# Softmax of the attention stage: a chained scaled minimum as bias, and the row sum's reciprocal as a power on GpSimd

## Chip, cores, metric

The kernel runs on one core of a Trainium2 chip, as one launch. The metric is device microseconds of one execution, the median of several runs. Five engines work side by side, each through its own instruction queue in order, and wait for one another by semaphores: TensorE (PE; its weight loads are PEld), VectorE (DVE), ScalarE (ACT), GpSimd (POOL), SyncE (SP, which here only issues DMAs).

## The reference

One layer of a hybrid block: 16 meta tokens and 1024 tokens (1040 rows, width 1024) go through a norm, then a "forgetting attention" and a diagonal state-space model side by side, then a gated merge, an output projection and a gated convolutional feed-forward. What the change touches is the attention, 8 heads of 64:

```
log_f = log_sigmoid(f_logit + b_forget);  cum_f = cumsum(log_f)
s = (q . k) / sqrt(64) + cum_f[t] - cum_f[s]        # s <= t, else -1e30
p = softmax(s, axis=-1)
out = p @ v
```

`cum_f[t]` is the same along a row, so it falls out of the softmax, and the kernel adds only the term of the key.

## The kernel before

All products are float32 made of two parts: a value is split into a high half (`hi`, rounded to the matmul type) and a low half (`lo`, what is left), and three matmuls make one product. The split is the pair that stands all over the trace: a copy on ScalarE to the high half and a subtraction on VectorE for the low half (`split_lo`, L125).

The program goes through its stages one after the other: norm, state-space model, gates, the gated linear unit, values, **attention** (about 378 to 645 us of the span), merge, output projection, norm, feed-forward. In attention the outer loop runs over four pairs of heads, the inner one over ten units of a pair: one unit for the 16 meta tokens of each head, then four units per head of two chunks of 128 queries each. A pair has 18 chunks, the stage 72. `scores(...)` of a unit is called before `second(...)` (which calls `pv`) of the unit before it, so that a unit's softmax runs while PE works at something else.

`scores` does this for a chunk of 128 queries and `kc` keys (16, 144, 272, ... 1040):

- GpSimd copies the queries to `qz` (L620) and cuts the mask into the diagonal block of the forget row: `fm` (L622, affine select).
- PE makes the scores into a PSUM tile `sp` (two buffers), in one to three blocks of at most 512 keys (L632, L633).
- VectorE goes over each block in one or two pieces (the part left of the diagonal with `fb`, the diagonal with `fm`): L638 adds the forget term, writes the sum to `pt` and the piece's largest value to a column of `mx`. In the trace that is a CUSTOM_DVE and a DVE_READ_ACCUMULATOR2 for each piece. A chunk has one to four pieces, all chunks together 184.
- VectorE takes the largest of the columns (L643, where there is more than one: 64 chunks) and multiplies it by -0.125 (L644): `nm[:, 1]`.
- ScalarE computes exp(0.125 * pt + nm) with the row sum (L645, an ACTIVATE and an ACTIVATION_READ_ACCUMULATOR).
- VectorE takes the reciprocal of the sum (L646), GpSimd multiplies the row by it (L647).

`pv` then takes the groups of one or two key blocks: PE transposes them to `tp` (L675), ScalarE casts `tp` to `th` (L682), VectorE subtracts to `tl` (L125), PE multiplies with the values: the high half (L696, reads `th`) and the low half (L697, reads `tl`), both into `po`. Between groups `fill` hands PE projection matmuls (L145 to L147, tile `mm`) of the next pair's queries and keys and of the merge gates; their weights are split by GpSimd (L135 `whi`, L125 `wlo`), and GpSimd also finishes the gates (L365 `gs`).

The order of instructions on each engine is not the order of the code: the framework's scheduler lists them by its own simulated timeline, under the data dependencies and a few manual ones ("spread", which ties the fill matmuls to marks a few groups back).

Of the kernel before, what the change touches and what calls it, by code (L numbers as in the profile page):

```python
# [9 lines left out]
F = mybir.dt.float32  # L10
# [3 lines left out]
AF = mybir.ActivationFunctionType  # L14
ALU = mybir.AluOpType
AX = mybir.AxisListType
# [3 lines left out]
P = 128  # L20
# [27 lines left out]
def block_kernel(ctx, tc, x, meta, g1, w_q, w_k, w_v, w_f, w_u, w_g, b_f, w_ao, lam_d, bw_d, cw_d,  # L48
                 d_sk, l_dt, w_glu, w_o, g2, w_up, cwt_d, w_dn, gf, out, dbg=None, upto=99):
    nc = tc.nc  # L50
    dbg = dbg or {}
    out = out[0]

    V, S, GP, PE, SY = nc.vector, nc.scalar, nc.gpsimd, nc.tensor, nc.sync

    def pool(stack, name, bufs=1, side=None, **k):
        return stack.enter_context(
            tc.tile_pool(name=name, bufs=bufs, side=side, reuse_waits="tile", **k))

    cp = pool(ctx, "const", side="left")  # L60
# [7 lines left out]
    def mm_ps():  # L68
        mm_n[0] += 1
        if mm_n[1] and mm_n[0] % 4 == 0:  # L70
            return po_ps()
        return pp.tile([P, 512], F, tag="mm", name="mm", bufs=3)
# [4 lines left out]
    def s_ps(name="sp"):  # L77
        return pp.tile([P, 512], F, tag="sp", name=name, bufs=2)
# [9 lines left out]

    ident = cp.tile([P, P], F, name="ident")
    make_identity(nc, ident)  # L90
    nhalf = cp.tile([P, 1], F, name="nhalf")
    V.memset(nhalf, -0.5)
    one = cp.tile([P, 1], F, name="one")
    V.memset(one, 1.0)


    u_d = dp.tile([SW // P, P, P // GC, NCH], F, name="u_d")
# [506 lines left out]
    ap = pool(st_a, "attn", side="left")  # L604
# [6 lines left out]
    def scores(t_, e, c, fb):  # L611
        t, n = TILES[c]
        kc = KS[c]
        Qs, Ks = t_[f"q{e}"], t_[f"k{e}"]
        hr = slice(64 * e, 64 * e + 64)
        m_ = max(n, 32)
        dg = kc - n

        qz = qzero[e][c % 2]
        GP.tensor_copy(qz[hr, :m_], Qs[hr, t:t + m_].bitcast(F))  # L620
        fm = ap.tile([P, P], F, tag="fm", name="fm", bufs=2)
        GP.affine_select(out=fm[:n, :n], in_=fb[:n, dg:kc], pattern=[[-1, n]],  # L622
                         compare_op=ALU.is_ge, fill=-1e30, base=0, channel_multiplier=1)
        pt = ap.tile([P, L], F, tag="pt", name="pt", bufs=4)
        mx = ap.tile([P, 4], F, tag="mx", name="mx", bufs=4)
        nb = -(-kc // 512)
        w = -(-kc // nb // 8) * 8
        ns = 0
        for b in range(nb):
            a0, a1 = b * w, min(kc, b * w + w)  # L630
            ps = s_ps()
            PE.matmul(ps[:m_, :a1 - a0], Qs[:, t:t + m_], Ks[:, a0:a1], start=True, stop=False)  # L632
            PE.matmul(ps[:m_, :a1 - a0], qz[:, :m_], t_["kl"][:, a0:a1], start=False, stop=True)  # L633
            for lo, hi, src in ((a0, min(a1, dg), fb), (max(a0, dg), a1, None)):
                if hi <= lo:
                    continue
                s_ = fb[:n, lo:hi] if src is not None else fm[:n, lo - dg:hi - dg]
                V.tensor_tensor_reduce(out=pt[:n, lo:hi], in0=ps[:n, lo - a0:hi - a0], in1=s_, scale=1.0,  # L638
                                       scalar=-3e38, op0=ALU.add, op1=ALU.max, accum_out=mx[:n, ns:ns + 1])
                ns += 1  # L640
        nm = ap.tile([P, 4], F, tag="nm", name="nm", bufs=4)
        if ns > 1:
            V.reduce_max(nm[:n, 0:1], mx[:n, :ns], axis=AX.X)  # L643
        V.tensor_scalar(nm[:n, 1:2], nm[:n, 0:1] if ns > 1 else mx[:n, :1], -0.125, None, ALU.mult)  # L644
        S.activation(pt[:n, :kc], pt[:n, :kc], AF.Exp, bias=nm[:n, 1:2], scale=0.125, accum_out=nm[:n, 2:3])  # L645
        V.reciprocal(nm[:n, 3:4], nm[:n, 2:3])  # L646
        GP.tensor_scalar(pt[:n, :kc], pt[:n, :kc], nm[:n, 3:4], 1.0, ALU.mult, ALU.mult)  # L647
        return pt

    def pv(h, cs, pts, ob):  # L650
# [81 lines left out]
    for pr in range(H // 2):  # L732
# [46 lines left out]
        for cs, e in units:  # L779
            pts = [scores(qk, e, c, fbs[e]) for c in cs]  # L780
            if prev:
                second(*prev)
            prev = (cs, e, pts)
# [47 lines left out]
    for i in range(KD):  # L831
# [3 lines left out]
        for t, n in QBLK:  # L835
            ps = mm_ps()
# [27 lines left out]
    for hf in range(2):  # L864
        woh, wol = wo[hf]
        sl = slice(512 * hf, 512 * hf + 512)
        for c, (t, n) in enumerate([(T0, 2)] + TILES[1:]):
            dst = hm if c == 0 else h2[:, c - 1]
            ps = mm_ps()
# [747 lines left out]
```

## Time and profile before

| | |
|---|---|
| median of 3 runs | 1508.43 us (1506.48 to 1508.51) |
| the profiled execution | 1508.38 us, of which the span of its instructions is 1506.6 us |
| PE busy | 1453.2 us, 96% of the span (weight loads 1366.2, 91%) |
| DVE busy | 1063.1 us, 71%, 2243 instructions |
| ACT busy | 677.9 us, 45% |
| POOL busy | 681.9 us, 45%, 759 instructions |
| chain that ended last, by engine | PE 80%, DVE 8%, DMA 3%, issue 3%, POOL 2%, ACT 2% |

How to read it: a share of busy time is a mean over stages. An engine that is busy for less than the whole of a stage costs time only where something waits for it, and what waits is read from the chain of work that ended last (which goes back from the last instruction, at each step to what released it) and from the idle times with what ended them. Matmuls are pipelined, so a row of PE overlaps the next, and a small gap can hide behind the end of the one before. The time of an execution is about 1.8 us more than its span.

### The profile page before, as it was taken

To read this page: it belongs to the slowest core of one execution; us is meant where nothing else is said; L and a number is where in the kernel's file an instruction comes from. 1 tells how busy PE (TensorE), PEld (TensorE's weight loads), DVE (VectorE), ACT (ScalarE), POOL (GpSimd) and SP (SyncE) were. 2 spreads that over 40 slices of the span, in tenths; PEclk is the share of its full clock that TensorE was granted. 3 is DMA by queue.
4 is the path that set the end of the run, shared out by engine and by line. 5 is a ranking of instruction groups with operands and counts; after the bars stand their busy time and mean duration, and the time that the engine had idled before them with its cause. 6 is when DMAs were issued, how large, how long until landed. Compare 5 with 4: busy or idle time off the path is not lost.

```text
span 1506.6 us, 26221 instructions
## 1 busy us (share of the span) xinstructions
PE 1453.2 (96%) x9637; PEld 1366.2 (91%) x9637; DVE 1063.1 (71%) x2243; ACT 677.9 (45%) x1322; POOL 681.9 (45%) x759
## 2 busy tenths in 40 slices
PE   5999998999999999999999899999999999989997
PEld 4999997998999999999778899999999999778885
DVE  7989567861657676656255988888777775788785
ACT  6256555531646565532033444444444444444333
POOL 2010004760645555525011644555543326599766
PEclk9999999999999999999999999999999999999998
DMA  5365642551021202157241146776642214873413
GB/s 213 86 152 154 140 123 87 165 159 41 28 74 49 78 24 91 43 190 256 88 163 61 51 111 161 196 190 185 162 124 84 79 63 162 302 228 126 139 44 112
DMA packets 82805, 187.74 MB, mean 125 GB/s; under 512 B 13594, under 2 KB 26538, under 8 KB 82324
## 3 DMA queue, kind: packets, MB, share of 16 engines
q1 hardware_dynamic: 68180, 155.49, 31.5%
q0 software_dynamic: 8704, 19.98, 7.5%
q10 hardware_dynamic: 5792, 10.60, 1.9%
q8 instruction: 76, 1.25, 0.3%
q14 instruction: 53, 0.43, 0.1%
HBM read 146.95 MB, written 60.96 MB: 138 GB/s over the span
## 4 chain that ended last, share of the span: by engine, by line
PE 80%; DVE 8%; DMA 3%; issue 3%; POOL 2%; ACT 2%; SPq 0%; POOLq 0%; ACTq 0%; DVEq 0%
PE mm L147 5%; PE mm L145 5%; PE mm L146 5%; PE sp L202 4%; PE sp L201 4%; PE sp L203 4%; PE tp L201 3%; PE tp L202 3%; PE tp L203 3%; PE mm L203 3%; PE mm L201 3%; PE mm L202 3%; PE tp L675 2%; PE po L697 2%; PE po L696 2%
## 5 line engine op out<-in xcount | busy, mean ns | idle before, releaser
L145 PE MATMUL mm<-xhi,whi 128*128 128x342 f32 (+2 forms) x584 | 191.6, 329 | 1.0 <-DVE q L125 1.0
L146 PE MATMUL mm<-xlo,whi 128*128 128x342 f32 (+2 forms) x584 | 190.1, 326 | 1.4 <-DVE xlo L125 1.4
L147 PE MATMUL mm<-xhi,wlo 128*128 128x342 f32 (+2 forms) x584 | 190.6, 327 | 0.4 <-DMA wlo<-in_w_g_dram 0.4
L146 PEld LDWEIGHTS mm<-xlo,whi 128*128 128x128 f32 x584 | 111.2, 190 | 2.1 <-DVE xlo L125 1.7
L145 PEld LDWEIGHTS mm<-xhi,whi 128*128 128x128 f32 x584 | 111.2, 191 | 1.9 <-PE sp L633 0.8
L147 PEld LDWEIGHTS mm<-xhi,wlo 128*128 128x128 f32 x584 | 111.0, 190 | 1.3 <-DMA wlo<-in_w_g_dram 0.6
L958 POOL TENSOR_TENSOR ov<-ov,og 128x1024 f32<-128x1024 f32 x21 | 51.3, 2442 | 130.7 <-ACT og L957 127.9
L125 DVE TENSOR_TENSOR sw<-sf,sw 128x512 fp32r<-128x512 f32 x76 | 70.7, 930 | 53.3 <-ACT sw L927 53.1
L927 ACT CAST sw<-sf 128x512 fp32r<-128x512 f32 x76 | 47.4, 624 | 113.1 <-POOL sf L935 82.1
L201 PE MATMUL mm<-xhi,sw 128*128 128x256 f32 (+1 forms) x304 | 85.4, 281 | 0.8 <-DVE ov L982 0.8
L203 PE MATMUL mm<-xhi,sw 128*128 128x256 f32 (+1 forms) x304 | 85.5, 281 | 0.0
L202 PE MATMUL mm<-xlo,sw 128*128 128x256 f32 (+1 forms) x304 | 85.2, 280 | 0.0
L682 ACT CAST th<-tp 128x256 fp32r<-128x256 f32 (+3 forms) x120 | 56.1, 472 | 62.1 <-PE tp L675 29.1
L125 DVE TENSOR_TENSOR tl<-tp,th 128x256 fp32r<-128x256 f32 (+3 forms) x120 | 65.2, 547 | 25.9 <-ACT th L682 24.5
L927 ACT CAST sw<-raw 128x512 fp32r<-128x512 f32 x69 | 42.3, 620 | 87.1 <-DMA raw<-in_w_up_dram 36.5
L1018 DVE SCALAR_TENSOR_TENSOR ov<-hv,cwt,ov 128x1024 f32<-128x1024 f32 x38 | 76.8, 2021 | 0.4 <-ACT ov L1016 0.4
L647 POOL TENSOR_SCALAR pt<-pt,nm 128x144 f32<-128x144 f32 (+4 forms) x72 | 51.0, 710 | 52.9 <-DVE nm L646 51.7
L935 POOL TENSOR_TENSOR sf<-raw,sf 128x512 f32<-128x512 f32 x38 | 62.7, 1649 | 23.0 <-DVE sw L125 23.0
L935 POOL TENSOR_TENSOR sf<-raw 128x512 f32<-128x512 f32 x38 | 50.6, 1332 | 48.2 <-DMA raw<-in_w_up_dram 20.4
L645 ACT ACTIVATE pt<-pt,nm 128x144 f32<-128x144 f32 (+4 forms) x72 | 52.9, 736 | 26.0 <-DVE nm L644 25.6
L638 DVE CUSTOM_DVE_ANT_0 pt<-sp,fb 128x328 f32<-128x328 f32 (+8 forms) x112 | 46.4, 430 | 20.6 <-PE sp L633 12.2
L163 POOL TENSOR_TENSOR rs<-vr,nhalf 128x1 f32<-128x1 f32 (+2 forms) x18 | 10.5, 594 | 110.1 <-PE mm L879 52.4
(589 smaller groups left out, 5444.2 us busy)
## 6 DMA issues: line engine op xcount, KB each, us to landing
raw<-in_w_up_dram SPq DMA_DIRECT2D x44, 512.0 KB, 3.8
t_d<-in_w_dn_dram POOLq DMA_DIRECT2D x44, 256.0 KB, 6.9
ar<-a_d SPq DMA_DIRECT2D x44, 256.0 KB, 4.6
wr<-t_d SPq DMA_DIRECT2D x44, 256.0 KB, 2.9
a_d<-ov SPq DMA_DIRECT2D x21, 512.0 KB, 2.6
wr<-in_w_dn_dram SPq DMA_DIRECT2D x33, 256.0 KB, 3.6
t_d<-in_w_dn_dram SPq DMA_DIRECT2D x22, 256.0 KB, 4.6
t_d<-t_d SPq DMA_DIRECT2D x22, 256.0 KB, 4.9
```

The source lines that it names most:

```text
L125: return eng.tensor_tensor(out_, src, hi.bitcast(F), ALU.subtract)
L145: yield PE.matmul(ps, whi[:, i, :], ahi[:, i], start=(i == 0), stop=False)
L146: yield PE.matmul(ps, whi[:, i, :], alo[:, i], start=False, stop=False)
L147: yield PE.matmul(ps, wlo[:, i, :], ahi[:, i], start=False, stop=(i == k - 1))
L201: PE.matmul(ps, a[0][:, i], bh, start=(i == 0 and not joins), stop=False, skip_group_check=True)
L202: PE.matmul(ps, a[0][:, i], bl, start=False, stop=False, skip_group_check=True)
L203: PE.matmul(ps, a[1][:, i], bh, start=False, stop=(i == kh - 1), skip_group_check=True)
L645: S.activation(pt[:n, :kc], pt[:n, :kc], AF.Exp, bias=nm[:n, 1:2], scale=0.125, accum_out=nm[:n, 2:3])
L682: S.copy(th[:kn, z:tw], tp[:kn, z:tw])
L927: S.copy(hi, src)
L935: sums.append(GP.tensor_tensor(f_, a, b, op))
L1018: V.scalar_tensor_tensor(out=o, in0=h_[:, j:SEQ + j], scalar=cwc(j, m), in1=o, op0=ALU.mult, op1=ALU.add)
```

## The change

The scores' pieces are now scaled by -0.125 as they leave PSUM, and each takes a running minimum: a piece starts from the column that the piece before it wrote (the first from 3e38) and writes its own. The last column is the minimum of the whole row, which is the negated scaled maximum, and goes into the exponential as its bias directly; the scale there is -1. The reduction over the columns and the multiplication by -0.125 are gone. The reciprocal of the row sum is now a power with exponent -1 on GpSimd, ahead of the multiplication that uses it. The constants are one tile of three columns.

```diff
-    nhalf = cp.tile([P, 1], F, name="nhalf")
-    V.memset(nhalf, -0.5)
-    one = cp.tile([P, 1], F, name="one")
-    V.memset(one, 1.0)
+    consts = cp.tile([P, 3], F, name="consts")
+    nhalf, one, minus = (consts[:, i:i + 1] for i in range(3))
+    for c_, v_ in ((nhalf, -0.5), (one, 1.0), (minus, -1.0)):
+        V.memset(c_, v_)
...
-                V.tensor_tensor_reduce(out=pt[:n, lo:hi], in0=ps[:n, lo - a0:hi - a0], in1=s_, scale=1.0,
-                                       scalar=-3e38, op0=ALU.add, op1=ALU.max, accum_out=mx[:n, ns:ns + 1])
+                V.tensor_tensor_reduce(out=pt[:n, lo:hi], in0=ps[:n, lo - a0:hi - a0], in1=s_, scale=-0.125,
+                                       scalar=mx[:n, ns - 1:ns] if ns else 3e38, op0=ALU.add, op1=ALU.min,
+                                       accum_out=mx[:n, ns:ns + 1])
                 ns += 1
-        nm = ap.tile([P, 4], F, tag="nm", name="nm", bufs=4)
-        if ns > 1:
-            V.reduce_max(nm[:n, 0:1], mx[:n, :ns], axis=AX.X)
-        V.tensor_scalar(nm[:n, 1:2], nm[:n, 0:1] if ns > 1 else mx[:n, :1], -0.125, None, ALU.mult)
-        S.activation(pt[:n, :kc], pt[:n, :kc], AF.Exp, bias=nm[:n, 1:2], scale=0.125, accum_out=nm[:n, 2:3])
-        V.reciprocal(nm[:n, 3:4], nm[:n, 2:3])
-        GP.tensor_scalar(pt[:n, :kc], pt[:n, :kc], nm[:n, 3:4], 1.0, ALU.mult, ALU.mult)
+        nm = ap.tile([P, 2], F, tag="nm", name="nm", bufs=4)
+        S.activation(pt[:n, :kc], pt[:n, :kc], AF.Exp, bias=mx[:n, ns - 1:ns], scale=-1.0, accum_out=nm[:n, :1])
+        GP.tensor_tensor(nm[:n, 1:2], nm[:n, :1], minus[:n], ALU.pow)
+        GP.tensor_scalar(pt[:n, :kc], pt[:n, :kc], nm[:n, 1:2], 1.0, ALU.mult, ALU.mult)
```

The changed file is two lines shorter: the exponential is L643 there, the power L644, the row's multiplication L645, the transposes L673, the products L694 and L695. Outside the attention stage the order on every engine is the same but for the constants' writes at the start; in it the scheduler lists much anew. Two engines, three places:

GpSimd, near the end of the first pair of heads, around the row of 1040 keys of the first head (`pt_4895` before, `pt_4867` now; `whi` and `wlo` are a projection's weights, `gs` a gate). Before:

```order
L680 MEMSET th_4972 128x128
L681 MEMSET tl_4973 128x128
L647 TENSOR_SCALAR pt_4895<-pt_4895,nm_4910 128x1040
L365 TENSOR_SCALAR gs_4837<-gs_4837 128x1026
L125 TENSOR_TENSOR wlo_5461<-raw_5458,whi_5460 128x1024
L620 CAST qz11_4146<-q1_4156 64x128
```

Now:

```order
L679 MEMSET tl_4943 128x128
L644 TENSOR_TENSOR nm_4882<-nm_4882,consts_71 128x1
L365 TENSOR_SCALAR gs_4811<-gs_4811 128x1026
L125 TENSOR_TENSOR wlo_5417<-raw_5414,whi_5416 128x1024
L645 TENSOR_SCALAR pt_4867<-pt_4867,nm_4882 128x1040
L620 CAST qz11_4146<-q1_4156 64x128
```

The power has the place of the multiplication, and the gate and the weights' low half now go between the two.

PE, in the first pair, where the rows of 400 and 528 keys of the first head are transposed (`tp_4509` and `tp_4516` before, `tp_4491` and `tp_4498` now; the products read the casts, `th_4418` of the unit before, `th_4494` of `tp_4491`). Before:

```order
L675 MATMUL tp_4516<-ident_66,pt_4379 128x128
L675 MATMUL tp_4509<-ident_66,pt_4397 128x128
L675 MATMUL tp_4516<-ident_66,pt_4397 128x128
L675 MATMUL tp_4516<-ident_66,pt_4379 128x128
L675 MATMUL tp_4516<-ident_66,pt_4397 128x128
L696 MATMUL po_4414<-th_4418,vt_3860 128x256
L697 MATMUL po_4414<-tl_4419,vt_3860 128x256
L696 MATMUL po_4414<-th_4426,vt_3860 128x256
```

Now:

```order
L673 MATMUL tp_4491<-ident_66,pt_4369 128x128
L673 MATMUL tp_4498<-ident_66,pt_4369 128x128
L673 MATMUL tp_4491<-ident_66,pt_4385 128x128
L673 MATMUL tp_4498<-ident_66,pt_4385 128x128
L673 MATMUL tp_4498<-ident_66,pt_4369 128x128
L673 MATMUL tp_4498<-ident_66,pt_4385 128x128
L694 MATMUL po_4490<-th_4494,vt_3860 128x256
L695 MATMUL po_4490<-tl_4495,vt_3860 128x256
```

Before, the products of the unit ahead stood behind the transposes; now the products of the same tile do, both halves within four instructions of its last transpose.

PE, at the start of the last unit's products, at the end of the stage (`tp_8376` before and `tp_8240` now are the second group, whose casts are `th_8381` and `th_8245`). Before, from the last three of the seven projection matmuls that follow `tp_8376`:

```order
L145 MATMUL mm_8408<-xhi_90,whi_8274 128x342
L146 MATMUL mm_8408<-xlo_91,whi_8274 128x342
L147 MATMUL mm_8408<-xhi_90,wlo_8275 128x342
L675 MATMUL tp_8394<-ident_66,pt_8208 128x128
L675 MATMUL tp_8394<-ident_66,pt_8230 128x128
L675 MATMUL tp_8394<-ident_66,pt_8208 128x128
L675 MATMUL tp_8394<-ident_66,pt_8230 128x128
L696 MATMUL po_8368<-th_8372,vt_3860 128x256
L697 MATMUL po_8368<-tl_8373,vt_3860 128x256
L696 MATMUL po_8368<-th_8381,vt_3860 128x256
L697 MATMUL po_8368<-tl_8382,vt_3860 128x256
```

Now, from the last transpose of `tp_8240`:

```order
L673 MATMUL tp_8240<-ident_66,pt_8096 128x128
L146 MATMUL mm_8272<-xlo_91,whi_8138 128x342
L147 MATMUL mm_8272<-xhi_90,wlo_8139 128x342
L694 MATMUL po_8232<-th_8236,vt_3860 128x256
L695 MATMUL po_8232<-tl_8237,vt_3860 128x256
L673 MATMUL tp_8258<-ident_66,pt_8076 128x128
L673 MATMUL tp_8258<-ident_66,pt_8096 128x128
L673 MATMUL tp_8258<-ident_66,pt_8076 128x128
L673 MATMUL tp_8258<-ident_66,pt_8096 128x128
L694 MATMUL po_8232<-th_8245,vt_3860 128x256
L695 MATMUL po_8232<-tl_8246,vt_3860 128x256
```

Two projection matmuls are left between the group's transposes and what follows, where there were seven.

## Rows read from the trace of the kernel before

**Rows 1.** Engines' busy time in stretches (from:to us, busy us and instructions), attention stage.

```profile
core 0: us, PE busy (x) PEld busy (x) DVE busy (x) ACT busy (x) POOL busy (x), PEclk, DMA share, GB/s
378.00:645.00 267.00, 264.16 (x1840) 257.33 (x1839) 175.06 (x767) 154.66 (x375) 147.43 (x304) 1.00 0.17 55
```

**Rows 2.** Chain of work that ended last, 378 to 645 us, shares by line.

```profile
by line: PE mm L147 17.6%; PE mm L145 17.3%; PE mm L146 17.1%; PE tp L675 13.5%; PE po L696 8.4%; PE po L697 8.4%; PE sp L632 6.3%; PE sp L633 6.2%; DVE tl L125 1.3%; DVE q L125 1.1%; ACT th L682 1.0%; issue 0.8%; DVE pt L638 0.4%; ACT q L4
```

**Rows 3.** Instructions on tile `nm` (count: duration ns least/median/most).

```profile
L646 DVE RECIPROCAL nm<-nm x72: 141/164/168, 380.7 to 641.1; 128x1 f32<-128x1 f32 x64, 16x1 f32<-16x1 f32 x8
L643 DVE TENSOR_REDUCE nm<-mx x64: 131/152/158, 381.3 to 639.5; 128x1 f32<-128x3 f32 x32, 128x1 f32<-128x2 f32 x24, 128x1 f32<-128x4 f32 x8
L644 DVE TENSOR_SCALAR nm<-nm x64: 130/153/155, 381.5 to 639.6; 128x1 f32<-128x1 f32 x64
```

**Rows 4.** Instructions of L638, its accumulator reads: one for each piece.

```profile
L638 DVE DVE_READ_ACCUMULATOR2_ANT mx<- x184: 71/83/86, 378.4 to 639.3; 128x1 f32 x176, 16x1 f32 x8
```

**Rows 5.** Who waited for whom, 378 to 645 us (us in total, times, longest).

```profile
POOL pt L647 <- DVE nm L646: 51.7, 40, 5.3
...
DVE nm L646 <- ACT pt L645: 24.4, 42, 1.3
```

**Rows 6.** Instructions of L163, the norms' power on GpSimd.

```profile
L163 POOL TENSOR_TENSOR rs<-vr,nhalf x18: 549/554/1109, 10.7 to 816.6; 128x1 f32<-128x1 f32 x16, 16x1 f32<-16x1 f32 x1, 2x1 f32<-2x1 f32 x1
```

**Rows 7.** VectorE in order of time (start us, us), one chunk's last pieces.

```profile
467.86 0.08 DVE L638 DVE_READ_ACCUMULATOR2_ANT mx<- 128x1 f32 x1
467.86 0.28 DVE L638 CUSTOM_DVE_ANT_0 pt<-sp,fm 128x128 f32<-128x128 f32 x1
468.07 0.08 DVE L638 DVE_READ_ACCUMULATOR2_ANT mx<- 128x1 f32 x1
468.19 0.16 DVE L643 TENSOR_REDUCE nm<-mx 128x1 f32<-128x3 f32 x1
```

**Rows 8.** All engines in order of time, one row of 272 keys from exponential to transpose.

```profile
453.96 0.18 ACT L645 ACTIVATION_READ_ACCUMULATOR pt<-pt,nm 128x1 f32 x1
...
454.17 0.16 DVE L646 RECIPROCAL nm<-nm 128x1 f32<-128x1 f32 x1 [0.34 <-ACT pt L645]
...
454.94 0.49 POOL L647 TENSOR_SCALAR pt<-pt,nm 128x272 f32<-128x272 f32 x1
...
457.05 0.38 PE L675 MATMUL tp<-ident,pt 128*128 128x128 f32 x2
```

**Rows 9.** Chain in order of time, 415.5 to 418 us: a group of 256 columns.

```profile
415.47 0.16 PE mm L147
...
416.04 0.12 PE tp L675
...
416.24 0.38 ACT th L682
...
416.65 0.44 DVE tl L125
...
417.13 0.39 PE po L697
```

**Rows 10.** The same, 448.8 to 451 us: a group of 512 columns.

```profile
449.13 0.59 ACT th L682
...
449.74 0.70 DVE tl L125
...
450.87 0.12 PE po L696
```

**Rows 11.** GpSimd at the end of the first pair, and PE's first transpose of its row.

```profile
429.88 1.16 POOL L647 TENSOR_SCALAR pt<-pt,nm 128x1040 f32<-128x1040 f32 x1
430.99 1.09 POOL L365 TENSOR_SCALAR gs<-gs 128x1026 f32<-128x1026 f32 x1
432.01 2.43 POOL L125 TENSOR_TENSOR wlo<-raw,whi 128x1024 fp32r<-128x1024 f32 x1
...
434.05 0.38 PE L675 MATMUL tp<-ident,pt 128*128 128x128 f32 x2
```

## The prediction

> **What bounds the kernel now.** I read the page first: TensorE is busy for 96% of the span and holds 80% of the chain that ended last. So a saving on another engine is worth something only where TensorE waits for that engine. The change touches the attention stage alone, so I cut the stage out: of its 267.0 us TensorE is busy for 264.16 at full granted clock, VectorE for 175.06, GpSimd for 147.43 [rows 1]. The busy share flatters TensorE, because the end of a matmul hides a small gap behind it. The chain inside the stage is stricter: the eight lines of TensorE hold 94.8%, so 5.2% of 267.0, or 13.9 us, is the most that anything but TensorE's own work costs there. VectorE's part is 1.3% in the low halves of the probabilities (3.5 us), 1.1% in those of the queries (2.9), 0.4% in the score pieces (1.1) [rows 2]. The instructions that the change removes, L643, L644 and L646, are not among the lines shown.
>
> **VectorE.** It loses 72 reciprocals of 164 ns, 64 reductions of 152 and 72 multiplications of about 153 [rows 3]: 11.8 + 9.7 + 11.0 = 32.5 us. It also loses the waits in which a reciprocal stood at the head of its queue until the exponential was done, 24.4 us in 42 cases [rows 5]. It gains a dependency: there are 184 pieces in 72 chunks [rows 4], so 112 pieces now start from what the piece before them wrote. Without one, a piece starts together with the accumulator read in front of it (both at 467.86); the reduction, which needs such a read, starts 0.12 us after it (468.07, 468.19) [rows 7]. 112 x 0.12 = 13.4 us of gaps at most, less where the scheduler puts something between. Net, VectorE gains some 19 us of time in the stage, besides the waits.
>
> The Trainium skill, page "VectorE: DVE Perf Modes", section "The DRAIN you can't avoid", says that a semaphore between chained VectorE operations costs nothing extra, by which the 13.4 us would be 0 and VectorE's gain 32.5 us. The rows just named show 0.12 us for it here.
>
> What of this reaches the end? Little. On the chain the low halves follow their ScalarE cast at once: the cast of 416.24 ends at 416.62, the subtraction starts at 416.65; that of 449.13 ends at 449.72, the next starts at 449.74 [rows 9, 10]. VectorE was free when it was asked, so an emptier queue starts them no sooner. Only the score pieces stand on the chain because VectorE is behind, for 1.1 us in all. Bounds: nothing, and all of VectorE's part on the chain (7.5 us) or, allowing for the casts just measured, some 4 us. I take -0.5, half of the pieces' part, as that is the row nearest to what is removed.
>
> **GpSimd.** It gains 72 powers of one column. The same operation runs 18 times in the norms, at 549 ns least, 554 median and one of 1109 [rows 6]. 72 x 0.554 = 39.9 us, so GpSimd goes from 147 to some 187 us of the stage's 267, still with room. Bounds of one power are 0.55 and 1.11; I take the median, since 17 of 18 lie by it.
>
> The Trainium skill, "GPSIMD Engine Reference", section 4.1 "Engine selection", speaks against this move: elementwise work belongs on VectorE, GpSimd being about twice as slow with two inputs. By that factor on the reciprocal's 164 ns a power would take an estimated 0.33 us and the sum be 24 us. The rows have it at 3.4 times the reciprocal.
>
> Is the row's multiplication late for the transposes? In the row of 272 keys the accumulator read ends at 454.14, the reciprocal at 454.33, GpSimd multiplies from 454.94 to 455.43, and TensorE takes the row at 457.05: 1.6 us in hand, the tightest that I found behind the stage's first 20 us [rows 8]. The new way to the end of the divisor is 0.55 instead of the 0.16 + 0.03 of reciprocal and hand-over, so 0.4 us later; the exponential itself starts sooner by reduction and multiplication (0.3 us) and later by up to three chained gaps (0.4). Altogether -0.3 to +0.5 us, within 1.6. GpSimd stood at the head of its queue for a reciprocal for 51.7 us already [rows 5]; the power waits there for the exponential instead, so `qz`, `fm` and the weights behind it wait no longer than before.
>
> In one place the order puts more than the power ahead of a row: the row of 1040 keys at the first pair's end now goes behind a gate (1.09) and a weights' low half (2.43), with the power 4.0 us in all. It was done at 431.04 and taken at 434.05, 3.0 us in hand; but the new order also lists its first transpose some 18 TensorE instructions later, at 0.16 us each 2.8 us [rows 9, 11]. 3.0 + 2.8 - 4.0 leaves 1.8. I take 0 for GpSimd. If that cover is gone at a few rows, some 3 us; that is the upper bound.
>
> **The new order on TensorE.** The amount of its work is the same; what counts is how far a product stands behind the transposes whose cast and subtraction it needs. A group of 256 columns needs from the end of the transpose (416.16) to the product of the low half (417.13) 0.97 us [rows 9]; one of 512 needs 0.59 + 0.70 and some 0.08 of hand-overs, 1.37 us [rows 10]. TensorE fills this at 0.12 us a transpose or product, 0.16 a projection matmul [rows 9, 10]. In the first order on TensorE shown with the change, three transposes and one product lie between the last transpose of `tp_4491` and its low half: 0.48 us, short by 0.5. In the other, the second group (`tp_8240`) has two projection matmuls, four transposes and three products: 0.32 + 0.48 + 0.36 = 1.16, short by 0.2; before there were seven matmuls, so none. A third place of the kind, in the first pair's last unit, comes out short by 0.4 (three transposes, one product, four score matmuls of 16 columns). Together +1.1 us. Bounds: 0, if a stall at one place only takes the place of another, and about 2.6, if ScalarE is behind and each comes to somewhat more than twice that.
>
> **Sum.** On the profiled execution, 1508.38 us (span 1506.6 and 1.8 around it), which is the median to 0.05: 1508.4 - 0.5 + 0 + 1.1 = 1509.0.
>
> **Rivals.** (1) *VectorE's relief reaches TensorE.* If emptier VectorE lets the score buffers, the queries' splits and the low halves go sooner after all, more than half of its 7.5 us on the chain goes: some -4 to -5, 1504. For it: these are the only waits in the stage that VectorE ends. Against it: the subtractions start 0.02 to 0.03 us after their casts [rows 9, 10]. Chance 0.15.
>
> (2) *Slower: GpSimd brings the rows late.* Two powers now often stand ahead of one multiplication. At 1.11 us each, the longest row, a row of the pair would be late by 2 x 1.11 and the 0.1 of slower start, 2.3 us against 1.6 in hand [rows 6, 8]: 0.7 us at each of the 32 larger units if nothing else moved, 22 us; with the transposes listed later by about a microsecond, as at the place worked out above, only the tightest quarter of them pays, 8 x 0.7 = 5.6 us: 1515. It decides from 0.8 us for a power (two make up the 1.6). Against it: 17 of 18 rows. Beside the page's advice on elementwise work named above this is the form in which that advice would cost time. Chance 0.08.
>
> (3) *Slower: the new order itself.* The same short places, each at the upper bound, and cover on GpSimd gone at a few rows: +2.6 and +3 at most, less the 0.5; some +4, 1512.5. Chance 0.15.
>
> (4) *The chained pieces hold VectorE up instead*: if all 13.4 us lay where TensorE waits for a score buffer, 1520; but 56 us of removed work and waits go from the same queue, so I leave it in the few per cent outside the range.
>
> **How the numbers follow.** About 0.2% or 3 us is what a measurement of this kernel can tell from no change. My forecast, 1509.0 with its own range 1506 to 1511.4, has 0.62. Faster by more than that: rival 1, 0.15. Slower: rivals 2 and 3, 0.23. The range reaches to rival 1's 1504 and past rival 3, to 1513.5, which is the sum with both upper bounds, 1508.4 - 0.5 + 2.6 + 3; rival 2 is left out at the top.
>
> **What will show it.** After the change: no L643 or L644 of the old kind and no reciprocal on VectorE, about 207 instructions fewer on it and its busy time some 32 us less; 72 powers of 0.55 us on GpSimd and 40 us more; a dependent piece starting about 0.12 us after the accumulator read. TensorE's busy time in the stage as before within 2 us, the stage's end within 2 us of where it was. Waits of TensorE for `tl` at the two places shown would prove the third term; idle time of TensorE that the multiplication on GpSimd ends would prove rival 2; a stage shorter by 4 us with the low halves' share gone, rival 1. I am wrong if the stages outside attention move, since no instruction there does.

## The result and the profile after

The changed kernel takes **1517.5 us** (median of four runs, 1517.05 to 1519.03) against 1508.47 for the kernel before: 1.0063 times the time, interval 1.0048 to 1.0078, or 9 us slower. The prediction was 1509.0 with a range of 1504.0 to 1513.5; the time lies above it.

The profiled execution took 1517.05 us, 1515.3 of them in its span. The page's busy times, and the attention stage's, in the columns of [rows 1]:

```profile
PE 1458.5 (96%) x9637; PEld 1368.6 (90%) x9637; DVE 1053.0 (69%) x2036; ACT 676.2 (45%) x1322; POOL 719.1 (47%) x831
```

```profile
378.00:645.00 267.00, 260.17 (x1789) 250.65 (x1788) 158.33 (x548) 148.79 (x367) 181.39 (x369) 1.00 0.18 55
```

GpSimd's gain, +37.2 us, is close to the forecast 40. VectorE has its 207 instructions fewer, but is busy for only 10.1 us less, where some 32 were forecast. In the same 267 us of span TensorE does 51 instructions and 4 us of work less than in [rows 1]: the loss is inside the stage. Its length is read from the line of the probabilities' transposes, whose row ends with the first and the last start. Before and after:

```profile
L675 PE MATMUL tp<-ident,pt x360: 178/272/330, 382.2 to 650.2; 128*128 128x128 f32 x176, 16*16 16x16 f32 x4
```

```profile
L673 PE MATMUL tp<-ident,pt x360: 178/272/329, 381.0 to 657.3; 128*128 128x128 f32 x176, 16*16 16x16 f32 x4
```

268.0 us became 276.3: **+8.3 of the span's +8.7** (1506.6 to 1515.3). Below, "the stage" is this stretch (the expectations of e9 to e11 count 0.27 us more, to the end of the last transpose), read from one profiled execution of each kernel. It is the better ruler, since the rest of an execution wanders by a few us (last section). The chain's shares in the stretch of [rows 2], after:

```profile
by line: PE mm L147 15.9%; PE mm L145 15.6%; PE mm L146 15.3%; PE tp L673 12.0%; PE po L695 8.2%; PE po L694 7.1%; PE sp L632 5.8%; PE sp L633 5.7%; issue 4.0%; DMA o_d<-ob 2.3%; DVE tl L125 1.5%; ACT th L680 1.2%; DVE pt L638 0.8%; DVE ob 
```

TensorE's eight lines fell from 94.8% to 85.6%. A transfer out of the output tile `ob` is new with 2.3%, and "issue" went from 0.8 to 4.0. Who TensorE itself waited for, 376 to 662 us (us in total, times, longest):

```profile
PE po L695 <- DVE tl L125: 2.2, 6, 0.7
PE po L694 <- DVE ob L699: 1.6, 3, 0.9
PE po L694 <- ACT th L680: 1.6, 5, 0.7
PE mm L145 <- DVE q L125: 1.0, 2, 0.5
```

Before, the same view has 1.4 for `tl`, 1.0 for `q`, 0.6 for a score buffer, and neither `th` nor `ob`. No transpose waits for GpSimd in this list: what is late are the products.

The power and the pieces, after, beside [rows 3, 4] (count: least/median/most, ns):

```profile
L644 POOL TENSOR_TENSOR nm<-nm,consts x72: 537/550/566, 379.6 to 648.0; 128x1 f32<-128x1 f32 x64, 16x1 f32<-16x1 f32 x8
...
L638 DVE CUSTOM_DVE_ANT_0 pt<-sp,fm,mx x64: 329/351/353, 379.4 to 646.1; 128x128 f32<-128x128 f32 x64
```

The power costs what the norms' power said. The piece of 128 columns, 286 ns before, now takes 351: that was not in the prediction at all.

### The profile page after: what moved, and what is told of

It reads as the page before. It is cut to its first block, busy times and chain, and to the rows that moved or that the text cites. A ratio compares the mean times of both kernels' runs of the same rounds, so it can differ in the third digit from the quotient of the medians.

```text
span 1515.3 us, 26160 instructions
## 1 busy us (share of the span) xinstructions
PE 1458.5 (96%) x9637; PEld 1368.6 (90%) x9637; DVE 1053.0 (69%) x2036; ACT 676.2 (45%) x1322; POOL 719.1 (47%) x831
## 4 chain that ended last, share of the span: by engine, by line
PE 77%; DVE 9%; issue 4%; DMA 4%; POOL 3%; ACT 2%; SPq 0%; POOLq 0%; DVEq 0%; ACTq 0%
PE mm L147 5%; PE mm L145 5%; PE mm L146 5%; PE sp L201 4%; PE sp L203 4%; PE sp L202 4%; PE tp L201 3%; PE tp L202 3%; PE tp L203 3%; PE mm L201 2%; PE mm L202 2%; PE mm L203 2%; PE tp L673 2%; PE po L695 2%; PE mm L877 1%
## 5 line engine op out<-in xcount | busy, mean ns | idle before, releaser
L202 PE MATMUL mm<-xlo,sw 128*128 128x256 f32 (+1 forms) x304 | 85.6, 281 | 0.0
L643 ACT ACTIVATE pt<-pt,mx 128x144 f32<-128x144 f32 (+4 forms) x72 | 53.0, 736 | 43.5 <-DVE mx L638 42.8
L163 POOL TENSOR_TENSOR rs<-vr,consts 128x1 f32<-128x1 f32 (+2 forms) x18 | 10.5, 591 | 109.3 <-PE mm L877 52.2
L694 PE MATMUL po<-th,vt 128*128 128x256 f32 (+1 forms) x200 | 57.0, 296 | 3.5 <-DVE ob L699 1.6
L673 PE MATMUL tp<-ident,pt 128*128 128x128 f32 (+1 forms) x360 | 59.3, 270 | 0.4 <-DVE tl L125 0.3
```

Source lines behind the costliest of these rows:

```text
L202: PE.matmul(ps, a[0][:, i], bl, start=False, stop=False, skip_group_check=True)
L673: PE.transpose(tp[:kn, o:o + n], p_[:n, k0:k0 + kn], ident[:n, :n])
L694: PE.matmul(po[:, :w], vt[:kn, kk, h, :], th[:kn, gi * w:gi * w + w], start=(kk == 0), stop=False)
```

## The experiments

**Theories.** O: the order that the scheduler made around the change costs the time, above all TensorE's. G: the power on GpSimd makes rows late. C: the chained pieces hold VectorE up. All of the runs at a glance (the ratio's interval is against the kernel before on the same chip):

| run | min | power | order in the stage | median us | interval of the ratio | stage us |
|---|---|---|---|---|---|---|
| before | - | - | own | 1507.4 to 1508.5 | | 268.0 |
| the change | chained | yes | own | 1517.5 | 1.0048 to 1.0078 | 276.3 |
| e1 | chained | - | own | 1510.0 | 0.9997 to 1.0018 | 268.8 |
| e2 | - | yes | own | 1515.0 | 1.0028 to 1.0058 | 273.5 |
| e3 | chained | yes | TensorE's of before | 1514.3 | 1.0020 to 1.0049 | 271.4 |
| e4 | - | - | TensorE's of the change | 1519.8 | 1.0050 to 1.0089 | 283.6 |
| e5 | chained | - | all of before | 1512.2 | 1.0013 to 1.0036 | 269.4 |
| e6 | - | yes | all of before | 1511.0 | 1.0008 to 1.0026 | 269.9 |
| e7 | chained | yes | all of before | 1510.8 | 1.0007 to 1.0030 | 272.2 |
| e8 | - | twice | all of before | 1524.1 | 1.0090 to 1.0125 | 283.9 |
| e9 | chained | yes | own, `ob` split | 1517.0 | 1.0041 to 1.0073 | 275.4 |
| e10 | unchained | - | all of before | 1508.4 | 0.9992 to 1.0010 | 267.7 |
| e11 | chained | yes | of before, gate last | 1509.7 | 1.0001 to 1.0028 | 270.5 |
| e12 | unchained, start from a tile | - | all of before | 1510.4 | 1.0009 to 1.0028 | 268.2 |

In e4, e7 and e8 a part of the stage ran at TensorE's lower granted clock, which lengthens it; in the others the stage's clock is 1.00 throughout.

### One half of the change at a time: e1 and e2

```diff
-        GP.tensor_tensor(nm[:n, 1:2], nm[:n, :1], minus[:n], ALU.pow)
+        V.reciprocal(nm[:n, 1:2], nm[:n, :1])
```

That is e1, from the changed kernel; e2 makes the opposite edit in the kernel before.

> The changed kernel with the reciprocal back on VectorE: the chained minimum alone. Theory A (the loss of 8.7 us is the order in which the scheduler now lists TensorE's work, products too near behind their transposes): this edit gives TensorE yet another list, so the time lies where that list puts it, anywhere from 1505 to 1518, and the loss shows as TensorE waiting for th, tl or ob. Rival B (the power on GpSimd brings the rows late): 1508, as before. Rival C (the chained pieces hold VectorE up): 1515 to 1518.

> The kernel before with the power on GpSimd alone; maximum, reduction and scaling as before. Theory A: again a list of its own, 1505 to 1518, with the loss, if any, in waits for th, tl or ob. Rival B: 1515 to 1518, with TensorE waiting for rows that GpSimd multiplies. Rival C: 1508.

Measured: the chained minimum alone 1510.0, no change that the interval tells from nothing; the power alone 1515.0. So most of the loss comes with the power. In e2 rival B has the number right and the reason wrong: TensorE waits for `tl` (2.9 us), for a score buffer (1.0) and for `ob` (0.9), and for no row that GpSimd multiplies. Each of the two also has an order of its own (TensorE's list differs from that of before at some 800 places in e1, at some 600 in e2), so a half's price and its order's are not yet apart.

### Orders exchanged: e3 and e4

TensorE's instructions of the stage are tied in a chain in the order of the other kernel, as dependencies without a semaphore:

```diff
+    for a_, b_ in zip(listed, listed[1:]):
+        tc.add_manual_dep(b_, a_.name, mybir.DependencyInfo(
+            mybir.DependencyClass.NoSync, mybir.DependencyReason.DATA), reason="order")
```

> The changed kernel, with TensorE's instructions of the attention stage held, one behind the other, in exactly the order that they have in the kernel before; the other engines are listed by the scheduler around it. Theory A: the loss goes, 1507 to 1510. Rivals B and C: the operations are what is late, so it stays, 1514 to 1519.

> The kernel before, with TensorE's instructions of the attention stage held in exactly the order of the changed kernel. Theory A: the loss comes with the order, 1514 to 1519. Rivals B and C: 1507 to 1510, as none of the changed operations is in it.

e3: 1514.3, the stage 271.4. With TensorE's order of before, the change loses 3.4 us in the stage instead of 8.3. What is left shows in TensorE's waits (376 to 662 us):

```profile
PE tp L673 <- POOL pt L645: 2.4, 3, 1.3
PE po L695 <- DVE tl L125: 2.2, 5, 1.1
```

Now transposes do wait for GpSimd, three times. Under the new order of TensorE the rows were in time and products were late; under the old one, with GpSimd listed anew, three rows are late too.

e4: 1519.8, even slower than the change, and **inconclusive** on the size of the order's cost. With TensorE's list fixed, the other engines were listed anew, and ScalarE put a gate that waited for a transfer out of the gates' tile in front of a cast. Behind it, and once before at 390.3 to 393.7 us, TensorE's granted clock is at its lower level, 0.50 (the windows below mix both levels); 10.2 us in all, which cost up to half of that. Chain in order of time, and the windows from there on (columns as [rows 1]):

```profile
435.94 5.26 DMA g_d<-gs
...
441.37 0.28 issue
441.65 0.38 ACT th L682
...
442.07 0.58 PE po L696
```

```profile
440.00:445.00 5.00, 2.93 (x13) 2.88 (x14) 1.65 (x5) 3.05 (x6) 1.10 (x2) 0.65 0.46 110
445.00:450.00 5.00, 5.00 (x27) 5.00 (x26) 1.08 (x2) 0.59 (x1) 0.47 (x2) 0.66 0.00 2
```

### All four engines held in the order of before: e5, e6, e7

The same chain of dependencies on TensorE, VectorE, ScalarE and GpSimd; instructions that are gone are left out of the lists, and each power stands directly ahead of its row's multiplication.

> The chained minimum alone (the reciprocal stays on VectorE), with the attention stage's instructions listed on TensorE, VectorE, ScalarE and GpSimd as in the kernel before (those that are gone left out). It shows at once what holding an order costs and what VectorE's relief brings without any new order. Theory 1 (the relief reaches nothing, the order was the rest): 1508.5, within 1 us of the kernel before, and the stalls of TensorE in the stage those of before. Theory 2 (VectorE's emptier queue does help TensorE, and the new order of the chained minimum alone, 1510.0, hid it): 1505 or less. Theory 3 (holding an order costs in itself): 1511 or more.

> The power on GpSimd alone, all four engines in the order of before, each power directly ahead of its row's multiplication. With a new order this edit took 1515.0. Theory 1 (the time is the order's; the power itself costs only where a row has little in hand): in the trace of before the time from the end of a row's multiplication to its first transpose is under 0.45 us for one row of 72 and under 1 us for three, so a delay of 0.39 to 0.55 us for a row costs 0.4 to 0.6 us, and 1.1 if the two rows of a unit add up: 1509 to 1509.6. Theory 2 (the power itself is the cost, whatever the order): 1512.5 to 1515.

> The whole change, all four engines in the order of before, each power directly ahead of its row's multiplication. With TensorE's order alone held it took 1514.3, with rows late from GpSimd for 2.4 us at three places. Theory 1 (those rows were late because other work stood between a power and its multiplication): 1508.5 to 1509.6, no transpose waiting for GpSimd but at the stage's start. Theory 2 (the power is the cost): 1512.5 or more, transposes waiting for GpSimd in the middle of the stage too.

Measured: 1512.2, 1511.0 and 1510.8; stages 269.4, 269.9 and 272.2. In the order of before the chained minimum costs 1.4 us in the stage, the power 1.9, both 4.2. But 4.2 is not the instructions' price alone. In the profiled execution of e7 TensorE's granted clock stood at its lower level, 0.50, from 391.8 to 395.2 us, after TensorE had been busy for only 2.5 of the 4 us from 388 on. e11 below has the same order there and the same 2.5 us, and kept 1.00. First e7, then e11 (columns as [rows 1]):

```profile
376.00:396.00 20.00, 17.37 (x98) 15.67 (x96) 8.24 (x41) 8.92 (x28) 14.64 (x36) 0.91 0.09 27
```

```profile
376.00:396.00 20.00, 17.37 (x111) 15.68 (x110) 9.92 (x49) 10.16 (x31) 16.06 (x40) 1.00 0.08 28
```

In the same busy time e7 does 98 instructions and e11 111. Counted from the first transpose, e7 is 1.6 us behind e11 after this stretch and still 1.0 us at 592. Without it e7's stage would be some 271.2 us and its price 3.3, which is that of e5 and e6 together. **The change's +8.3 is thus about 3.3 from its instructions and about 5.0 from the new order.** Most of the order's price comes with the power: the power alone has 273.5 in its own order (e2) and 269.9 in that of before, the minimum alone 268.8 (e1) and 269.4. e3, with TensorE's order alone from before and the other engines listed anew, has a stage about as short as e7's, so putting TensorE's order back is enough; the test the other way round, e4, failed. The medians agree in kind and are too wide for the split: e7 lies 1.1 to 4.5 us above the kernel before, e3 3.0 to 7.4, the change 7.2 to 11.8.

Theory 1 held for e6 and e7 only in its mechanism: the rows were late at the stage's start alone, but the sizes were too small. For e5 the time is theory 3's, but that holding an order costs nothing in itself is shown by e10 below; the relief helped nothing, nor was the chained minimum free. By medians e5 lies 2 to 3 us above what its stage explains; that part stands outside the stage (last section).

e6, who TensorE waited for:

```profile
PE po L697 <- DVE tl L125: 2.2, 5, 1.1
PE tp L675 <- POOL pt L647: 1.1, 2, 0.6
```

The two rows are at 381.7 and 395.9 us. In the trace of before the first of them, multiplied from 382.02, was done 0.05 us ahead of its first transpose, the other, from 395.01, 0.62 us; every other row there had 0.97 us or more. The 1.1 in one wait for `tl`, 0.3 before, is taken up with e11.

e5, VectorE in order of time, the chunk of [rows 7]:

```profile
467.71 0.36 DVE L638 CUSTOM_DVE_ANT_0 pt<-sp,fb,mx 128x136 f32<-128x136 f32 x1
468.00 0.08 DVE L638 DVE_READ_ACCUMULATOR2_ANT mx<- 128x1 f32 x1
468.23 0.35 DVE L638 CUSTOM_DVE_ANT_0 pt<-sp,fm,mx 128x128 f32<-128x128 f32 x1
468.50 0.08 DVE L638 DVE_READ_ACCUMULATOR2_ANT mx<- 128x1 f32 x1
```

The second piece starts 0.52 us after the first (467.71, 468.23). In the trace of before that distance is 0.22 (467.64, 467.86). So a dependent piece comes 0.30 us later and takes 0.065 more. The bias was ready there 0.89 us after the first piece's start (467.64 to 468.53, where the multiplication ends); here it is ready 0.87 us after (467.71 to 468.58): removing a reduction and a multiplication bought 0.02 us. Over the stage's 112 dependent pieces the start behind the accumulator read is 0.23 us in the median, against 0 before.

### The power twice: e8

```diff
-        GP.tensor_tensor(nm[:n, 3:4], nm[:n, 2:3], minus[:n], ALU.pow)
+        for _ in range(2):
+            GP.tensor_tensor(nm[:n, 3:4], nm[:n, 2:3], minus[:n], ALU.pow)
```

> As the power alone in the order of before, but each power issued twice, which doubles the suspected cost: a row is later by 0.94 us than with the reciprocal, the second of a unit by up to 1.9. From the time in hand of each row in the trace of before, 0.94 us would cost 1.4 us and 1.9 us would cost some 9. Theory 1 (the cost is the rows that run out of time in hand, and grows faster than the delay): 1510 to 1517, the added time standing as transposes that wait for GpSimd. Theory 2 (the power costs through something else, such as a shared port or the queues): twice the extra of the single power, with no such waits.

Measured: 1524.1, the stage 283.9. The first power cost 1.9 us in the stage, the second 14.0 more, and it stands where theory 1 put it:

```profile
PE tp L676 <- POOL pt L648: 9.9, 11, 1.6
```

Two late rows became eleven, from 1.1 us to 9.9. Another 1.5 us are products that wait for GpSimd's zero fills, and up to 1.7 of the 14.0 are the clock: after a wait of 1.4 us for a row, at 603, it stood at 0.50 from 604.3 to 607.7 us.

```profile
596.00:616.00 20.00, 17.51 (x107) 16.34 (x107) 8.35 (x51) 8.76 (x30) 18.19 (x42) 0.91 0.19 60
```

The mechanism is G's, and it grows faster than the delay; its size was again above the expectation of 1510 to 1517.

### The output tile: e9

```diff
-        mx = ap.tile([P, 4], F, tag="mx", name="mx", bufs=4)
+        mx = ap.tile([P, 6], F, tag="mx", name="mx", bufs=4)
...
-        nm = ap.tile([P, 2], F, tag="nm", name="nm", bufs=4)
+        nm = mx[:, 4:6]
...
-                obs[cs] = ap.tile([P, 256], F, tag="ob", name="ob", bufs=1)
+                w_ = sum(TILES[c][1] for c in cs)
+                obs[cs] = ap.tile([P, w_], F, tag=f"ob{w_}", name=f"ob{w_}", bufs=1)
```

In the changed kernel the chain has, at the start of the third pair:

```profile
525.66 0.43 DVE ob L699
...
526.11 3.52 DMA o_d<-ob
...
529.72 0.18 DVE ob L699
...
529.94 0.27 PE po L694
```

> The changed kernel, TensorE's order in the stage unchanged, but the output rows of the 16-query units get a tile of their own (the row sums share the tile of the minima, which makes the room), so that they no longer wait for the previous unit's transfer out of the only such tile. In the changed kernel TensorE loses 1.19 us at 528.7 and 0.46 at 460.6 behind that. Theory 1 (in the new order this wait is a cost of its own): the stage, first to last transpose, falls from 276.6 to about 275.0, the transfer out is gone from the chain, and the time is 1516. Theory 2 (another wait stands right behind it): the stage stays within 0.5 us of 276.6.

Measured: 1517.0, the stage 275.4, 0.9 us shorter. The wait for `ob` fell from 1.6 us in three cases to 0.4 in one and the transfer is gone from the chain; about half of what was removed was kept, so the answer lies between the two theories. It is one of several waits of the new order, not the whole of it.

### A better version?: e10 and e12

```diff
-                V.tensor_tensor_reduce(out=pt[:n, lo:hi], in0=ps[:n, lo - a0:hi - a0], in1=s_, scale=1.0,
-                                       scalar=-3e38, op0=ALU.add, op1=ALU.max, accum_out=mx[:n, ns:ns + 1])
+                V.tensor_tensor_reduce(out=pt[:n, lo:hi], in0=ps[:n, lo - a0:hi - a0], in1=s_, scale=-0.125,
+                                       scalar=3e38, op0=ALU.add, op1=ALU.min, accum_out=mx[:n, ns:ns + 1])
...
-            V.reduce_max(nm[:n, 0:1], mx[:n, :ns], axis=AX.X)
-        V.tensor_scalar(nm[:n, 1:2], nm[:n, 0:1] if ns > 1 else mx[:n, :1], -0.125, None, ALU.mult)
-        S.activation(pt[:n, :kc], pt[:n, :kc], AF.Exp, bias=nm[:n, 1:2], scale=0.125, accum_out=nm[:n, 2:3])
+            V.tensor_reduce(out=nm[:n, 0:1], in_=mx[:n, :ns], op=ALU.min, axis=AX.X)
+        S.activation(pt[:n, :kc], pt[:n, :kc], AF.Exp, bias=nm[:n, 0:1] if ns > 1 else mx[:n, :1], scale=-1.0,
+                     accum_out=nm[:n, 2:3])
```

e12 is e10 with `scalar=top[:n] if ns else 3e38`, where `top` is a column of 3e38 in the tile of constants.

> A version meant to beat both: the pieces are scaled and take a minimum as in the change, but each from a constant start, so none waits for another; one reduction over the columns gives the bias, only the multiplication is gone, and the reciprocal stays on VectorE; all engines in the order of before. Theory 1 (the chaining made the pieces dearer: 65 ns each for the start value read from a tile and some 0.13 us of wait, which ate what the removed instructions gave): the pieces are back at 286 ns for 128 columns, VectorE's busy time is some 10 us under that of before, the stage 267 to 268.5 us against 268.2, the time within 1.5 us of before. Theory 2 (holding the order is what made the chained version 4 us slower than before): 1511 or more here too.

> As the unchained minimum in the order of before (1508.4), but every piece after a chunk's first takes its start value from a constant column of a tile instead of an immediate, so that it has the chain's operand and not the chain's wait. It parts the two prices of the chained piece: 351 ns against 286 for 128 columns, and a start 0.23 us after the start of the accumulator read instead of together with it. Theory 1 (the operand costs the 65 ns, the dependency the later start): pieces of 351 ns that start together with the read ahead of them, the stage between that of the unchained version (267.7 from the first transpose's start to the last one's) and that of the chained one (269.4). Theory 2 (both come from the dependency): 286 ns, stage 267.7. Theory 3 (both come from the operand): 351 ns and a start 0.2 us behind the read's, stage 269.4.

e10 took 1508.4, the stage 267.7: the kernel before, within what can be told. VectorE's 72 multiplications are gone for nothing, since TensorE did not wait for them; but nothing is lost either, so holding the order is free. It ties with the kernel before and does not beat it. e12's pieces:

```profile
L638 DVE CUSTOM_DVE_ANT_0 pt<-sp,fm,consts x64: 340/347/351, 379.5 to 637.9; 128x128 f32<-128x128 f32 x64
```

```profile
466.70 0.08 DVE L638 DVE_READ_ACCUMULATOR2_ANT mx<- 128x1 f32 x1
466.70 0.35 DVE L638 CUSTOM_DVE_ANT_0 pt<-sp,fm,consts 128x128 f32<-128x128 f32 x1
```

347 ns, where e10's take 286, and the piece starts together with the read ahead of it: the start value from a tile costs the 61 ns, the dependency the later start. Theory 1. Its stage is 268.2; its median, 1510.4, is above that by 2 to 3 us outside the stage, as e5's is.

### The gate behind the zero fills: e11

The lists of e7, but at the stage's end GpSimd's `gs` goes behind two fills:

```diff
 L135 TENSOR_SCALAR whi
-L365 TENSOR_SCALAR gs
 L678 MEMSET th
 L679 MEMSET tl
+L365 TENSOR_SCALAR gs
```

> The whole change in the order of before, as in the earlier run of it (1510.8), but at the stage's end GpSimd finishes the gate behind the two zero fills instead of ahead of them, so that it is not at work when VectorE splits the weights of the merge. Theory 1 (that split, 128x512 with both inputs in SBUF, takes 0.69 us when it starts ahead of GpSimd's gate and 1.3 to 1.6 when it starts during it, and the last low halves come late for that): the split takes 0.69, TensorE's wait for the low half there falls from 1.29 to about 0.4 us, the stage from 272.5 to 271.6. Theory 2 (the split is slow for another reason): it stays at 1.3 us or more.

GpSimd and VectorE at that place, before:

```profile
648.18 1.56 POOL L365 TENSOR_SCALAR gs<-gs 128x1026 f32<-128x1026 f32 x1
```

```profile
648.13 0.69 DVE L125 TENSOR_TENSOR wlo<-raw,whi 128x512 fp32r<-128x512 f32 x1 [0.23 <-POOL whi L135]
```

In e7, and in e11:

```profile
651.49 1.05 POOL L365 TENSOR_SCALAR gs<-gs 128x1026 f32<-128x1026 f32 x1
651.50 1.57 DVE L125 TENSOR_TENSOR wlo<-raw,whi 128x512 fp32r<-128x512 f32 x1 [0.25 <-PE po L694]
...
653.73 0.39 PE L695 MATMUL po<-tl,vt 128*128 128x256 f32 x1 [1.14 <-DVE tl L125]
```

```profile
650.11 0.69 DVE L125 TENSOR_TENSOR wlo<-raw,whi 128x512 fp32r<-128x512 f32 x1 [0.25 <-PE po L694]
```

Theory 1: 0.69 us, TensorE's loss there back at 0.4, the stage 270.5, by 1.7 us shorter (0.8 to 0.9 here; the rest is what e7 lost at the lower clock). Before, the split started 0.05 us ahead of the gate and the gate waited; in e7 it started 0.01 us behind, and the split waited, with two `tl` behind it on VectorE and TensorE behind those. The Trainium skill, page "SBUF — State Buffer", section "Who interferes with whom", says that a VectorE instruction with two SBUF inputs contends with a GpSimd instruction that reads SBUF, and that the order of issue decides which of the two is held up. These rows agree: 0.69 against 1.57, decided by a few hundredths of a microsecond.

## Why the prediction was wrong, point by point

**What bounds the kernel** was right: TensorE, and in the attention stage alone; the rest of the span differs by 0.4 us (1.2 less ahead of the stage, 1.5 more behind it).

**VectorE, -0.5.** Wrong, in sign too. The price of a chained piece was read as 0.12 us of wait [rows 7]; it is 0.30 us of later start and 0.065 us of longer work. By an estimate from that one chunk 112 x 0.30 is 33.6 us, all of the 32.5 that were removed. The step that failed is taking the reduction's distance behind an accumulator read for that of a piece: a piece otherwise overlaps the one ahead of it, and gives up the overlap as well. The sentence of the Trainium skill weighed there (page "VectorE: DVE Perf Modes", section "The DRAIN you can't avoid": between eight copies in a row a semaphore costs nothing extra) does not carry over to these pieces: it is further off here than the 0.12 us was. In the order of before the chained minimum costs 1.4 us (e5); C, and rival 4 with its 13.4 us, had the mechanism and five to ten times the size. Rival 1 is out: every version with less on VectorE kept a stage of 267.7 us or more.

**GpSimd, 0.** The price of one power was right (0.550), and so was the place worked out, the row of 1040 keys behind a gate and a weights' half: done at 435.06, taken at 437.38, 2.3 us in hand against the forecast 1.8. What failed is the search for the tightest row: it began behind the stage's first 20 us, and the two rows that pay stand in them. With the shared ports at the stage's end, 0.9 us, which the prediction did not consider, the term is +1.9 (e6) instead of 0, within its upper bound of 3. Rival 2 did not happen at 0.55 us a power, but its point was well put: at twice that (e8) eleven rows are late and the stage is 14 us longer than with one.

**The new order on TensorE, +1.1, at most 2.6.** This is the largest miss: about 5.0 us (4.1 against e7 as it was profiled, 5.0 without its stretch at the lower clock). The three places were real, but two of them cost more, because another engine was not free:

- At `tp_4491`, forecast 0.5: 0.67 us ahead of the high half and 0.44 ahead of the low one, 1.1 in all. VectorE had two splits of the next keys, an output tile and a score piece before it, as the changed kernel's chain shows:

```profile
397.82 0.31 DVE kl L125
...
398.27 0.44 DVE kl L125
...
398.74 0.42 DVE ob L699
...
399.56 0.35 DVE tl L125
...
399.95 0.39 PE po L695
```

- At `tp_8240`, forecast 0.2: 0.82, from the weights' split that GpSimd's gate slowed:

```profile
654.67 1.33 DVE wlo L125
656.00 0.61 DVE tl L125
...
656.65 0.39 PE po L695
```

- The third, forecast 0.4: 0.44, though for a score buffer and not for a low half.

Together 2.4, inside the bound of 2.6. What the bound did not hold is the places that were not looked at: the output tile's transfer (1.19 us at 528.7 and 0.46 at 460.6), two late casts of some 0.4 us at 486.6 and 555.5, and smaller ones. Not every loss counts, since some only take the place of one that the old order has too: 0.90 us for a cast at 387.6, where before TensorE loses 0.89 at 388.4 to a score buffer; 0.6 for each of two low halves at 519.2 and 589.4, where before it loses 0.5 each at 516.6 and 583.4. The failed step is to let three places stand for an order that differs from that of before at over a thousand. "VectorE was free when it was asked" held for the old order [rows 9, 10], and the new one took away just that.

**The sum.** -0.5 + 0 + 1.1 = +0.6 against +1.4, +1.9 and about +5.0, or +8.3 in the stage. All three terms were too small. Rival 3, the new order at its bounds with cover lost on GpSimd, was the right kind of case; 1512.5 was too near.

## What to carry to other kernels

When a scheduler lists a stage anew, hold the old order with dependencies to price the edit apart from the order; here the order cost more than the edit. Here instructions removed from an engine that is not the bottleneck were worth nothing, while a dependency added between instructions that overlapped before took up all that they had taken. Look at the granted clock of each stretch before two stages are compared: in e7 a short fall looks like a cost of the instructions. Look for the tightest row at a stage's start, where buffers and queues are still filling, and count who shares ports with work that is moved to GpSimd.

## What the runs showed of the hardware

- A VectorE piece with a start value from a tile takes 347 to 351 ns for 128 columns, 286 with an immediate (e12, e5; before, e10).
- A piece that starts from the value that the piece ahead wrote begins 0.23 us after the start of the accumulator read, one without it together with the read (e5, e12).
- A two-input split on VectorE takes 0.69 us, or 1.57 if a GpSimd instruction got ahead of it by 0.01 us (before, e7).
- In e4, after TensorE idled for 2.7 us waiting for a cast, its granted clock stood at 0.65 and 0.66 from 440 to 450 us, and is 1.00 in the windows on both sides. After like idle times it fell in the profiled execution of e7 (391.8 to 395.2 us) and not in that of e11.
- After the stage the granted clock falls in some places, and not equally in each execution, with the same instructions in the same order there. Three stretches of 20 us at the same distances from the end, before and in e7:

```profile
846.60:866.60 20.00, 15.48 (x84) 15.31 (x84) 19.96 (x24) 8.29 (x14) 16.87 (x11) 0.83 0.34 100
1266.60:1286.60 20.00, 17.65 (x86) 16.23 (x87) 15.40 (x21) 10.66 (x19) 10.81 (x8) 0.91 0.29 93
1326.60:1346.60 20.00, 16.15 (x66) 12.93 (x65) 17.22 (x18) 8.71 (x16) 20.00 (x13) 0.91 0.71 223
```

```profile
848.80:868.80 20.00, 15.64 (x90) 15.47 (x89) 19.96 (x23) 6.73 (x12) 16.92 (x11) 0.91 0.27 82
1268.80:1288.80 20.00, 17.35 (x95) 15.74 (x94) 14.96 (x21) 10.71 (x19) 12.96 (x9) 1.00 0.34 104
1328.80:1348.80 20.00, 15.98 (x65) 12.78 (x65) 17.22 (x18) 8.67 (x16) 20.00 (x13) 0.91 0.74 223
```

The span behind the last transpose was 856.4 us before and 854.4 in e7; added up over the granted clock of that stretch, TensorE stood at its lower level for 21 us of it before and 14.5 in e7. In e5 it is 27 us of 859.6, in e12 30 of 862.1. Half of the time at that level is lost, so the clock accounts for about 3 of e5's 3.2 us and 4 of e12's 5.7 behind the stage, as profiled. It is not the only thing that wanders there: e9 has 21 us too, and 860.3. This is why the stage's length says more here than the total. The 2 to 3 us that e5 and e12 have outside the stage by their medians are not settled by it: over all its executions e5's mean granted clock is 0.9912 against 0.9918 before, which is worth less than 1 us.
